# The modulation products of a two-layer diffusion step: thinner beside mLSTM heads 2 to 4, the rest beside the next stage, weights in two tiles of their own

## The chip, the cores and the metric

One core of one Trainium2 chip runs the whole program in one launch. The metric is device time in microseconds, from runs of the same program: the median of three runs before is 1559.02 us (1558.22 to 1560.73). One further execution was taken by the hardware profiler; all views below are of that one.

## The reference

Two layers of a hybrid backbone over 1024 latent tokens and 128 context tokens, model width 1024, all in float32. Layer 0 has four mLSTM heads (two directions, chunks of 128 tokens) and eight grouped-query attention heads from one input projection; layer 1 has 16 heads of 2-D neighbourhood attention. Around each layer stand RMS norms with a shift, a scale and a gate that come from a conditioning vector, one for the latent tokens (`c`) and one for the context (`c_ctx`):

```
m = jnp.dot(jax.nn.silu(cvec), w) + b          # w: (1024, 3072) for each layer
sh, sc, gt = jnp.split(m, 3, axis=-1)
h = rmsnorm(x, g_pre) * (1.0 + sc) + sh
x = x + gt * rmsnorm(y, g_post)
```

Shift and scale of layer 0 are needed before the first projection. The other four vectors (gate of layer 0; shift, scale and gate of layer 1), for both conditioning vectors, are needed only after layer 0's attention. They are what this case is about: 4 x 1024 outputs, each a product of 1024 weights with the vector, twice.

## The kernel before, in words

**Stages.** `run` opens one phase after the other: "front" (norm of the input, first shift and scale, first projections of head 1), "a" (gates of the mLSTM, rest of head 1's projections, first two of head 2), "mlstm" (four heads), "g" (silu gates of the attention heads, keys, values and queries), "gqa" (attention), "out0" (output projection of layer 0, norm into layer 1), "na" (layer 1 and its output). Activations are kept transposed in 9 x 2 tiles as a high and a low part; a projection is 8 blocks of the width times 3 matmuls (high x high, low x high, high x low) into one accumulator bank (`feat_part`, L371 to L373), for one of three chunks of 384 tokens at a time. Two banks (`pj`) take turns, so a projection can start only when the one two before it has been read out.

**The mLSTM phase.** Head by head: `mlstm` runs the recurrence over 8 chunks in both directions (`kw` on POOL in L670, two matmuls in L673, the state's update on VectorE in L680), then three groups of three chunks with the decays (`e`, L653 to L658), the scores and values (L710 to L719), the norm of the result (L725 to L739) and its gating (L750). Between two heads `blocks` projects for the next ones: of head h+1 the values, the output gate and the silu gate, of head h+2 the queries and keys; that is 9 and 6 projections, three to each. The silu gate takes a half-step on ScalarE (L395), one on POOL (L396) and a product on VectorE that reads the bank (L397). The start state of a head is copied in L638 (`mlstm_start`).

**The modulation products.** `mods_rest` is a generator. A step loads 256 rows of the transposed weights (`wm`, 128 x 2 x 512, 512 KB, on SP's queue, L238) and makes four products with sums on VectorE (L252; the sum is read out by a second instruction of the same line), two blocks of rows by two conditioning vectors, which lie broadcast in `cb` (L245). 32 steps cover two halves of the width, 16 each; the load for a step is issued one step ahead. `blocks` asks the generator for a step after every projection, so that the steps come beside heads 2 and 3 and the first of head 4. After the 32nd step the ends follow at once: `mod` sums the halves (L256), `mod_end` adds the bias, applies gains, and for the two gates transposes on PE (L225) and stores rows to DRAM (`ggd`, L228).

**Memory.** Most tiles come from one pool of 35 slots of 4.6 KB per partition (`u`): the 18 activation tiles, queries, keys, values and gates of the heads in work, high and low parts of projection weights, and `wm`. Each phase has a pool of its own (`t`), laid on the memory of the phase before it; a tile there waits only for the tiles that it lies on (`reuse_waits="tile"`). `("e", 3, ...)` and `("nr", 3, ...)` are made first in their phases.

**Order.** The program is written in the order above, and the framework plans the order on each engine and queue from it (`schedule_with_timeline_sim=True`): an instruction can come earlier than its place when its inputs and its tile are ready. Only PE's order in the attention of "gqa" and in the last products of `na_pair` is written out by hand.

**Phase "g".** `zb` projects four blocks of the silu gate, three chunks each, into `gz`, which goes to DRAM; `gqa_kv` projects and normalises keys and values token block by token block (`norm_rope`, tile `nr`, L785 to L791; `key_stack`, L808 to L810), `gqa_q` the queries, twice.

Of the kernel before, what the change touches and what calls it, by code (L numbers as in the profile page):

```python
# [13 lines left out]
ALU = mybir.AluOpType  # L14
# [4 lines left out]
P = 128  # L19
D = 1024  # L20
KB = D // P
T = 1152
NT = 9
NC = 3
CW = 384
# [14 lines left out]
class Kern:  # L40
# [186 lines left out]
            nc.vector.tensor_copy(rows, pt[:16, :P])  # L227
            nc.sync.dma_start(self.ggd[l].rearrange("k r p -> (k r) p"), rows)  # L228

    def mods_rest(self):  # L230

        nc, a = self.nc, self.a
        mp = self.const([P, 2, 4, KB, 2], "mp")
        junk = self.t("mj", 1, [P, 512])

        def load(hf, q):
            w = self.u([P, 2, 512], n="wm")
            nc.sync.dma_start(w.rearrange("p b k -> p (b k)"), a["w_modT"][hf, q])  # L238
            return w

        steps = [(hf, q) for hf in range(2) for q in range(16)]
        nxt = load(0, 0)
        for hf in range(2):
            cb = self.t("cb", 1, [P, 2, 512])
            nc.sync.dma_start(cb.rearrange("p r (k f) -> p r k f", f=P), self.csd.rearrange("(o r k) f -> o r k f", o=1, r=2)[:, :, 4 * hf : 4 * hf + 4, :].to_broadcast([P, 2, 4, P]))  # L245
            for q in range(16):
                w = nxt
                if 16 * hf + q < 31:
                    nxt = load(*steps[16 * hf + q + 1])
                for b in range(2):  # L250
                    for r in range(2):
                        nc.vector.tensor_tensor_reduce(junk, w[:, b, :], cb[:, r, :], 1.0, 0.0, ALU.mult, ALU.add, mp[:, hf, q // 4, 2 * (q % 4) + b, r : r + 1])  # L252
                yield
        for j, (l, kind) in enumerate(((0, 2), (1, 0), (1, 1), (1, 2))):
            m = self.const([P, KB, 2], f"mod{l}{kind}")
            nc.vector.tensor_tensor(m, mp[:, 0, j], mp[:, 1, j], ALU.add)  # L256
            self.mod_end(m, l, kind)
            if kind < 2:
                (self.shift, self.scale)[kind][l] = m
# [623 lines left out]
                nc.vector.tensor_tensor(lo, x, hi.bitcast(F32), ALU.subtract)  # L883
        return Q, ahead

    def zb(self, h):
        nc, a = self.nc, self.a
        for j in range(4):
            gz = self.u([P, T], n="gz")
            w = self.weights(a["w_ab"][20 + j], "lo")  # L890
            if j == 2:
                self.gqa_tables()
            if j == 3:
                ahead = self.gqa_weights(0)
            self.feat(h, w, lambda c, ps: self.silu_gate(gz[:, c * CW : (c + 1) * CW], ps))
            nc.scalar.dma_start(self.gzd[j], gz)
        return ahead

# [391 lines left out]
    def run(self):  # L1290
        nc, a = self.nc, self.a
        x = lambda i: a["x_sample"][i * P : (i + 1) * P, :] if i < 8 else a["x_prompt"]
        rest = iter(())

        def blocks(hd, evs, bs, new=None):
            for b in bs:
                w = self.weights(a["w_ab"][5 * hd + b], new=new)
                for c in range(NC):
                    self.feat(h, w, evs[b], [c])
                    next(rest, None)  # L1300

        with self.phase("front"):
            self.setup()
# [5 lines left out]
            h = [self.chunk("h") for _ in range(NC)]  # L1309
# [80 lines left out]
        with self.phase("mlstm", ("e", 3, [P, 4, CW])):  # L1390
            self.ts = [self.decays_load(0, g) for g in range(NC)]
            start = self.mlstm_start(0)
            rest = self.mods_rest()
            for hd in range(HA):
                self.mlstm(hd, *start, *pr())
                if hd < HA - 1:
# [6 lines left out]
            for _ in rest:  # L1403
                pass
        with self.phase("g", ("nr", 3, [P, 3, 256])):
            w = self.gqa_kv(h, self.zb(h))
            Q, early = [], []
            for g in range(2):
                q, w = self.gqa_q(h, g, w, Q, early)
                Q.append(q)  # L1410
        gz, w = w, []
        with self.phase("gqa"):
            self.pt = self.ring("pt", 14)
# [4 lines left out]
        h = []  # L1418
# [216 lines left out]
```

## Time and profile before

| | us |
|---|---|
| median of three runs (lowest to highest) | 1559.02 (1558.22 to 1560.73) |
| the profiled execution | 1557.34 |
| its span, first to last instruction | 1555.5 |
| PE busy | 1501.9 |
| VectorE (DVE) busy | 852.4 |
| ScalarE (ACT) busy | 653.9 |
| GpSimd (POOL) busy | 605.0 |
| products' first instruction, 128 of them, busy | 110.7 |

The profile gives for each engine how long it was busy, for groups of equal instructions how often they ran and how long one took, and what ended the idle time before them (`<-`, with the engine, tile and line that released it). PEld is the loading of weights into TensorE, which overlaps its matmuls. Stretches are given as start and end in us from the span's start; behind the busy times stand PE's granted clock as a share of full speed, the DMA engines' busy share and GB/s.

### The profile page before, as it was taken

The numbers are of one execution on the slowest core, as the hardware profiler recorded it, in microseconds if no ns is written. First come the engines' busy times: TensorE is split into PE (matmuls) and PEld (weight loads), VectorE is DVE, ScalarE is ACT, GpSimd is POOL, SyncE is SP. The second block draws the span as 40 slices with busy tenths as digits, with TensorE's granted clock in tenths as the row PEclk, the third lists the DMA queues.
The fourth block names the chain that finished last, engine by engine and source line by source line (L and its number), as shares of the span: only waits on it lengthen the run. The fifth ranks groups of instructions, "written<-read, shape, count | busy, mean of one in ns | idle before, by whom it ended". The sixth has DMA issues, their size and how long they took to land.

```text
span 1555.5 us, 27151 instructions
## 1 busy us (share of the span) xinstructions
PE 1501.9 (97%) x10164; PEld 1378.2 (89%) x10164; DVE 852.4 (55%) x2346; ACT 653.9 (42%) x1573; POOL 605.0 (39%) x826
## 2 busy tenths in 40 slices
PE   7899989999999899999999999999999999999998
PEld 5799988999999887777788989999999999989886
DVE  5732897974547946676465452435243434345532
ACT  4622212222235767787344452445243434355411
POOL 3414644644445835675123332333142314243200
PEclk9999999999999999999999999999999999999999
DMA  9112534432221000121334212131213121225342
GB/s 361 74 42 100 218 126 170 163 106 78 99 97 32 16 23 32 37 95 30 102 119 148 89 52 82 39 104 25 92 44 97 31 84 37 88 75 155 123 130 81
DMA packets 75011, 143.80 MB, mean 92 GB/s; under 512 B 15928, under 2 KB 46848, under 8 KB 74880
## 3 DMA queue, kind: packets, MB, share of 16 engines
q1 hardware_dynamic: 70294, 126.91, 24.5%
q10 hardware_dynamic: 4586, 15.16, 2.6%
q8 instruction: 80, 1.31, 0.3%
q14 instruction: 51, 0.42, 0.1%
HBM read 115.47 MB, written 21.86 MB: 88 GB/s over the span
## 4 chain that ended last, share of the span: by engine, by line
PE 83%; DVE 7%; ACT 3%; issue 2%; POOL 2%; DMA 1%; SPq 0%; DVEq 0%; POOLq 0%; ACTq 0%
PE pj L371 12%; PE pj L373 12%; PE pj L372 12%; PE pj L387 7%; PE pj L386 7%; PE pj L388 7%; PE ptr L106 4%; PE o L1285 4%; PE s L1262 3%; PE o L954 3%; PE tr L106 3%; PE s L914 3%; DVE mj L252 2%; PE pj L106 2%; DVE pr L915 1%
## 5 line engine op out<-in xcount | busy, mean ns | idle before, releaser
L371 PE MATMUL pj<-hh,whi 128*128 128x384 f32 x1168 | 399.6, 342 | 4.1 <-DVE z L397 3.8
L373 PE MATMUL pj<-hh,wlo 128*128 128x384 f32 x1168 | 396.4, 340 | 0.0
L372 PE MATMUL pj<-hl,whi 128*128 128x384 f32 x1168 | 395.6, 339 | 0.0
L371 PEld LDWEIGHTS pj<-hh,whi 128*128 128x128 f32 x1168 | 219.5, 188 | 7.3 <-DVE z L397 2.9
L372 PEld LDWEIGHTS pj<-hl,whi 128*128 128x128 f32 x1168 | 219.6, 188 | 1.3
L373 PEld LDWEIGHTS pj<-hh,wlo 128*128 128x128 f32 x1168 | 219.3, 188 | 1.2 <-issue 0.5
L115 POOL TENSOR_TENSOR wlo<-raw,whi 128x1024 fp32r<-128x1024 f32 (+1 forms) x71 | 146.6, 2075 | 155.2 <-ACT whi L114 124.4
L1272 POOL TENSOR_SCALAR sb<-sb,sm 128x512 f32<-128x512 f32 (+1 forms) x128 | 84.8, 668 | 241.2 <-DVE sm L1271 232.7
L924 POOL TENSOR_SCALAR pr<-pr,smg 128x384 f32<-128x384 f32 x192 | 113.8, 611 | 83.2 <-DVE smg L922 57.5
L386 PE MATMUL pj<-whi,hh 128*128 128x256 f32 x432 | 122.4, 284 | 0.3 <-DVE nr L789 0.3
L387 PE MATMUL pj<-wlo,hh 128*128 128x256 f32 x432 | 122.4, 284 | 0.0
L388 PE MATMUL pj<-whi,hl 128*128 128x256 f32 x432 | 122.4, 284 | 0.0
L386 PE MATMUL pj<-whi,yh 128*128 128x512 f32 x288 | 114.2, 397 | 1.5 <-DVE o L1080 1.5
L915 DVE CUSTOM_DVE_ANT_0 pr<-s,zero 128x384 f32<-128x384 f32 x192 | 102.2, 552 | 24.2 <-PE s L914 23.2
L387 PE MATMUL pj<-wlo,yh 128*128 128x512 f32 x288 | 113.8, 395 | 0.0
L388 PE MATMUL pj<-whi,yl 128*128 128x512 f32 x288 | 113.5, 395 | 0.0
L252 DVE CUSTOM_DVE_ANT_0 mj<-wm,cb 128x512 f32<-128x512 f32 x128 | 110.7, 865 | 3.8 <-DMA wm<-in_w_modT_dram 1.8
L1270 ACT ACTIVATE sb<-sb,sm 128x512 f32<-128x512 f32 (+1 forms) x128 | 88.9, 695 | 52.0 <-DVE sm L1268 47.5
L914 PE MATMUL s<-Kst,Q 128*128 128x384 f32 x384 | 105.4, 370 | 4.6 <-DVE smg L915 3.7
L114 ACT CAST whi<-raw 128x1024 fp32r<-128x1024 f32 (+1 forms) x89 | 80.8, 929 | 21.0 <-DMA raw<-in_w_out_dram 6.2
L1268 DVE CUSTOM_DVE_ANT_1 sb<-s,bias 128x512 f32<-128x512 f32 (+1 forms) x112 | 73.0, 664 | 24.3 <-PE ptr L106 11.3
L921 ACT ACTIVATE pr<-pr,smg 128x1152 f32<-128x1152 f32 x64 | 81.0, 1265 | 4.6 <-DVE smg L919 4.1
(351 smaller groups left out, 2961.5 us busy)
## 6 DMA issues: line engine op xcount, KB each, us to landing
wm<-in_w_modT_dram SPq DMA_DIRECT2D x32, 512.0 KB, 5.9
raw<-in_w_c_dram SPq DMA_DIRECT2D x25, 512.0 KB, 3.6
raw<-in_w_ab_dram SPq DMA_DIRECT2D x20, 512.0 KB, 3.5
e<-rbd ACTq DMA_DIRECT2D x12, 768.0 KB, 6.5
bias<-in_na_bias_dram SPq DMA_DIRECT2D x16, 576.0 KB, 5.0
wm<-in_w_mod_dram SPq DMA_DIRECT2D x16, 512.0 KB, 7.1
raw<-in_w_out_dram SPq DMA_DIRECT2D x16, 512.0 KB, 3.6
y<-yd SPq DMA_DIRECT2D x18, 448.0 KB, 3.4
```

Of the source, the lines that this page charges most:

```text
L106: self.nc.tensor.transpose(out, in_, self.ident)
L115: (eng_lo or nc.gpsimd).tensor_tensor(lo, src, hi.bitcast(F32), ALU.subtract)
L252: nc.vector.tensor_tensor_reduce(junk, w[:, b, :], cb[:, r, :], 1.0, 0.0, ALU.mult, ALU.add, mp[:, hf, q // 4, 2 * (q % 4) + b, r : r + 1])
L371: nc.tensor.matmul(ps[:, :CW], a, hh, start=k == 0, stop=False)
L372: nc.tensor.matmul(ps[:, :CW], a, hl, start=False, stop=False)
L373: nc.tensor.matmul(ps[:, :CW], b, hh, start=False, stop=k == KB - 1)
L386: nc.tensor.matmul(ps[:, :width], hh, a, start=k == 0, stop=False)
L387: nc.tensor.matmul(ps[:, :width], hh, b, start=False, stop=False)
L388: nc.tensor.matmul(ps[:, :width], hl, a, start=False, stop=k == KB - 1)
L914: nc.tensor.matmul(s[:, :CW], x, y, start=part == 0, stop=part == 1)
L915: nc.vector.tensor_tensor_reduce(pr[:, c, :], s[:, :CW], zero, -1.0, -NEG, ALU.add, ALU.min, m3[:, c : c + 1])
L924: nc.gpsimd.tensor_scalar(pr[:, c, :], pr[:, c, :], r, 1.0, ALU.mult, ALU.mult)
```

## The change

`blocks` counts its projections in `self.tick` and asks for a step only when the count modulo 8 is under 5. The mLSTM phase gets steps 0 to 23, the phase "g" steps 24 to 31: there `zb` asks for one after the second and third chunk of each of its four blocks. The weights no longer take a slot for each step: two tiles, `wm0` and `wm1`, are made once and take turns, in the mLSTM phase from the slots, in "g" from that phase's own pool, as are `mj` (the products, which nobody reads) and `cb`, which is loaded once more there. The partial sums `mp` are made before the loop. The ends become a function of their own, `mods_end`, which is called after both groups of queries; its body is the old one.

```diff
-    def mods_rest(self):
+    def mods_rest(self, steps, new):
         nc, a = self.nc, self.a
-        mp = self.const([P, 2, 4, KB, 2], "mp")
+        mp = self.mp
         junk = self.t("mj", 1, [P, 512])
-
-        def load(hf, q):
-            w = self.u([P, 2, 512], n="wm")
-            nc.sync.dma_start(w.rearrange("p b k -> p (b k)"), a["w_modT"][hf, q])
+        ring = [new(f"wm{j}") for j in range(2)]
+
+        def load(s):
+            w = ring[s % 2]
+            nc.sync.dma_start(w.rearrange("p b k -> p (b k)"), a["w_modT"][s // 16, s % 16])
             return w
-        steps = [(hf, q) for hf in range(2) for q in range(16)]
-        nxt = load(0, 0)
-        for hf in range(2):
-            cb = self.t("cb", 1, [P, 2, 512])
-            nc.sync.dma_start(cb...)
-            for q in range(16):
-                w = nxt
-                if 16 * hf + q < 31:
-                    nxt = load(*steps[16 * hf + q + 1])
-                for b in range(2):
-                    for r in range(2):
-                        nc.vector.tensor_tensor_reduce(junk, w[:, b, :], cb[:, r, :], ...)
-                yield
+        nxt, old = load(steps[0]), None
+        for s in steps:
+            hf, q = divmod(s, 16)
+            if hf != old:
+                cb, old = self.t("cb", 1, [P, 2, 512]), hf
+                nc.sync.dma_start(cb...)
+            w = nxt
+            if s + 1 in steps:
+                nxt = load(s + 1)
+            for b in range(2):
+                for r in range(2):
+                    nc.vector.tensor_tensor_reduce(junk, w[:, b, :], cb[:, r, :], ...)
+            yield
+
+    def mods_end(self):
+        nc, mp = self.nc, self.mp
         for j, (l, kind) in enumerate(((0, 2), (1, 0), (1, 1), (1, 2))):
...
-    def zb(self, h):
+    def zb(self, h, rest):
...
-            self.feat(h, w, lambda c, ps: self.silu_gate(gz[:, c * CW : (c + 1) * CW], ps))
+            for c in range(NC):
+                self.feat(h, w, lambda c, ps: self.silu_gate(gz[:, c * CW : (c + 1) * CW], ps), [c])
+                if c:
+                    next(rest, None)
...
-        rest = iter(())
+        rest, self.tick = iter(()), 0
...
                     self.feat(h, w, evs[b], [c])
-                    next(rest, None)
+                    self.tick += 1
+                    if self.tick % 8 < 5:
+                        next(rest, None)
...
-            rest = self.mods_rest()
+            self.mp = self.const([P, 2, 4, KB, 2], "mp")
+            rest = self.mods_rest(range(24), lambda n: self.u([P, 2, 512], n=n))
...
         with self.phase("g", ("nr", 3, [P, 3, 256])):
-            w = self.gqa_kv(h, self.zb(h))
+            rest = self.mods_rest(range(24, 32), lambda n: self.t(n, 1, [P, 2, 512]))
+            w = self.gqa_kv(h, self.zb(h, rest))
+            for _ in rest:
+                pass
             Q, early = [], []
             for g in range(2):
                 q, w = self.gqa_q(h, g, w, Q, early)
                 Q.append(q)
+            self.mods_end()
```

More of the change, by code (lines that the diff above doesn't have):

```diff
@@ L228, in mod_end @@
             nc.sync.dma_start(self.ggd[l].rearrange("k r p -> (k r) p"), rows)
-    def mods_rest(self):
+    def mods_rest(self, steps, new):
         nc, a = self.nc, self.a
-        mp = self.const([P, 2, 4, KB, 2], "mp")
+        mp = self.mp
         junk = self.t("mj", 1, [P, 512])
-        def load(hf, q):
-            w = self.u([P, 2, 512], n="wm")
-            nc.sync.dma_start(w.rearrange("p b k -> p (b k)"), a["w_modT"][hf, q])
-            return w
-        steps = [(hf, q) for hf in range(2) for q in range(16)]
-        nxt = load(0, 0)
-        for hf in range(2):
-            cb = self.t("cb", 1, [P, 2, 512])
-            nc.sync.dma_start(cb.rearrange("p r (k f) -> p r k f", f=P), self.csd.rearrange("(o r k) f -> o r k f", o=1, r=2)[:, :, 4 * hf : 4 * hf + 4, :].to_broadcast([P, 2, 4, P]))
-            for q in range(16):
-                w = nxt
-                if 16 * hf + q < 31:
-                    nxt = load(*steps[16 * hf + q + 1])
-                for b in range(2):
-                    for r in range(2):
-                        nc.vector.tensor_tensor_reduce(junk, w[:, b, :], cb[:, r, :], 1.0, 0.0, ALU.mult, ALU.add, mp[:, hf, q // 4, 2 * (q % 4) + b, r : r + 1])
-                yield
+        ring = [new(f"wm{j}") for j in range(2)]
+        def load(s):
+            w = ring[s % 2]
+            nc.sync.dma_start(w.rearrange("p b k -> p (b k)"), a["w_modT"][s // 16, s % 16])
+            return w
+        nxt, old = load(steps[0]), None
[3 more added lines that the diff above has]
+                cb, old = self.t("cb", 1, [P, 2, 512]), hf
+                nc.sync.dma_start(cb.rearrange("p r (k f) -> p r k f", f=P), self.csd.rearrange("(o r k) f -> o r k f", o=1, r=2)[:, :, 4 * hf : 4 * hf + 4, :].to_broadcast([P, 2, 4, P]))
+            w = nxt
[3 more added lines that the diff above has]
+                for r in range(2):
+                    nc.vector.tensor_tensor_reduce(junk, w[:, b, :], cb[:, r, :], 1.0, 0.0, ALU.mult, ALU.add, mp[:, hf, q // 4, 2 * (q % 4) + b, r : r + 1])
+            yield
+    def mods_end(self):
+        nc, mp = self.nc, self.mp
         for j, (l, kind) in enumerate(((0, 2), (1, 0), (1, 1), (1, 2))):
```

## The prediction

> **What bounds the kernel now.** I read the page's totals first, then the busy time of each engine in stretches, cut where the start state of a head is copied (L638), then the products alone in the same stretches, then who waited for whom. The page, totals and the span in 40 slices:
>
> ```profile
> span 1555.5 us, 27151 instructions
> PE 1501.9 (97%) x10164; PEld 1378.2 (89%) x10164; DVE 852.4 (55%) x2346; ACT 653.9 (42%) x1573; POOL 605.0 (39%) x826
> PE   7899989999999899999999999999999999999998
> DVE  5732897974547946676465452435243434345532
> ```
>
> TensorE sets the end: it idles 53.6 us of the whole span (1555.5 - 1501.9), so no change elsewhere can give more. VectorE is at 55% over the span, but its slices 4 to 8 (155 to 350 us) hold 9, 7, 9, 7, 4: that is where the products are. The copies that part the stretches, then busy time in them (PE, PEld, DVE, ACT, POOL, PE's granted clock), and below it the products' first instruction alone:
>
> ```profile
> 148.94 0.49 DVE L638 COPY cs<-ptr 128x128 f32<-128x128 f32 x2 [1.83 <-PE ptr L106]
> ...
> 206.25 0.48 DVE L638 COPY cs<-ptr 128x128 f32<-128x128 f32 x2
> ...
> 294.36 0.48 DVE L638 COPY cs<-ptr 128x128 f32<-128x128 f32 x2
> ...
> 375.55 0.49 DVE L638 COPY cs<-ptr 128x128 f32<-128x128 f32 x2 [2.23 <-PE ptr L106]
> ```
>
> ```profile
> 149.20:206.30 57.10, 52.57 (x332) 50.75 (x333) 47.20 (x115) 12.57 (x39) 36.97 (x44) 0.98 0.46 167
> 206.30:294.40 88.10, 81.63 (x512) 79.81 (x511) 78.12 (x189) 18.34 (x50) 46.85 (x53) 1.00 0.47 169
> 294.40:375.80 81.40, 78.54 (x502) 77.39 (x501) 59.43 (x150) 18.08 (x50) 40.03 (x47) 1.00 0.33 116
> 375.80:447.00 71.20, 71.20 (x462) 71.03 (x461) 31.98 (x67) 15.66 (x49) 27.32 (x47) 1.00 0.27 95
> ```
>
> ```profile
> 149.20:206.30 57.10, 28.81 (x32) 0.98 0.46 167
> 206.30:294.40 88.10, 52.25 (x60) 1.00 0.47 169
> 294.40:375.80 81.40, 29.65 (x38) 1.00 0.33 116
> ```
>
> PE idles 4.53, 6.47, 2.86 and 0.00 us in the four, 13.86 together. A step is four products, so they hold 8, 15, 9.5 and 0 steps: **0.57, 0.43 and 0.30 us of PE idle for each step**. The second and third stretch do the same kind of work (512 and 502 matmuls); the one with 15 steps took 88.10 us, the one with 9.5 took 81.40. And in the third, the part after its last product (the first row has the first and last start) has no idle at all:
>
> ```profile
> L252 DVE CUSTOM_DVE_ANT_0 mj<-wm,cb x128: 673/692/2877, 158.8 to 342.2; 128x512 f32<-128x512 f32 x128
> ...
> 342.90:375.80 32.90, 32.90 (x216) 32.58 (x215) 16.39 (x36) 10.69 (x35) 21.11 (x27) 1.00 0.25 90
> ```
>
> What ended PE's idle time between 110 and 550 us, the longest (total, times, longest):
>
> ```profile
> PE pj L371 <- DVE z L397: 3.8, 3, 1.9
> PE o L673 <- POOL kw L670: 2.4, 2, 1.2
> PE tr L106 <- POOL hs L739: 2.1, 2, 1.3
> ```
>
> A projection waits for its accumulator bank, which the silu gate's product on VectorE empties (L397): that wait belongs to a VectorE that is behind. The two on POOL would stay, except as far as POOL is itself held up (below).
>
> **The change, part by part.** A step's price on VectorE, from the groups between 150 and 350 us (busy, mean ns), two products that follow each other undisturbed, and the weight loads (time from issue to landing):
>
> ```profile
> L252 DVE CUSTOM_DVE_ANT_0 mj<-wm,cb 128x512 f32<-128x512 f32 x128 | 110.7, 865 | 3.8 <-DMA wm<-in_w_modT_dram 1.8
> L252 DVE DVE_READ_ACCUMULATOR2_ANT mp<- 128x1 f32 x128 | 10.1, 79 | 0.0
> ...
> 223.39 0.69 DVE L252 CUSTOM_DVE_ANT_0 mj<-wm,cb 128x512 f32<-128x512 f32 x1
> 224.13 0.69 DVE L252 CUSTOM_DVE_ANT_0 mj<-wm,cb 128x512 f32<-128x512 f32 x1
> ...
> DMA to landing us min/median/max: 4.2/5.9/8.8
> ```
>
> Undisturbed, one product follows another after 0.74 us, so a step is 4 x 0.74 = 2.96; by the means it is 4 x (0.865 + 0.079) = 3.78.
>
> *Thinner steps beside heads 2 to 4.* The counter starts at 9 when the stage begins (3 + 6 projections in the stage before it), and a remainder under 5 of 8 lets a step pass. So the three stretches get 6, 9 and 9 steps in place of 8, 15 and 9.5 (by program place 9, 15 and 8). At the third stretch's price, 24 x 0.30 = 7.2 us of idle remain of 13.86: **-6.7**. I take that price because all three new densities (6 in 57, 9 in 82, 9 in 81 us) are nearest to that stretch's. The bounds: no idle at all, as after 342.9, gives -13.9; the first stretch's price gives 24 x 0.57 = 13.7, so -0.2.
>
> *Eight steps beside the next stage's gate projections* (two of three chunks of four blocks). In 375.8 to 447 VectorE is busy 31.98 of 71.20 us and PE never idles; eight steps are 8 x 2.96 = 23.7 and fit into the 39.2 that are free. Nothing can be gained where PE is never idle, so the lower bound is 0; the upper is worked out under the second rival (9.7). I take the price of the third stretch again, 8 x 0.30 = **+2.4**.
>
> [...] The row first: a product at 241.06 met POOL's low-half subtraction and took 2.88 us, and POOL's half-step of the silu gate (L396) is longer beside the products (149 to 294 us) than without them (376 to 447):
>
> ```profile
> 240.97 2.42 POOL L115 TENSOR_TENSOR wlo<-raw,whi 128x1024 fp32r<-128x1024 f32 x1 [0.24 <-ACT whi L114]
> 241.06 2.88 DVE L252 CUSTOM_DVE_ANT_0 mj<-wm,cb 128x512 f32<-128x512 f32 x1
> ...
> L396 POOL TENSOR_SCALAR th<-th 128x384 f32<-128x384 f32 x5 | 4.1, 821 | 5.7 <-ACT th L395 5.7
> L396 POOL TENSOR_SCALAR th<-th 128x384 f32<-128x384 f32 x14 | 7.9, 565 | 30.4 <-ACT th L395 29.0 <-issue 1.3
> ```
>
> [...]
>
> *Two tiles of their own.* The weights leave the 35 shared slots. Two waits for a slot by projection weights go, both off PE (who waited, for whom; total, times, longest):
>
> ```profile
> POOL wlo L115 <- DVE mp L252: 5.1, 1, 5.1
> ACT whi L114 <- DVE mp L252: 4.2, 2, 3.2
> ```
>
> In return two slots are held through the stage, which the old order held only when a load was near, and load s+1 may now start only when step s-1 is done: two steps in 5.9 + 2.96 us, 4.4 us each. That is under the time from one projection to the next, as the counts of L371, eight to a projection, give it: 57.10 us for 8.5 in the first stretch (6.7 each), 71.20 for 13 in the last (5.5 each):
>
> ```profile
> 149.20:206.30 57.10, 23.32 (x68) 12.82 (x69) 0.98 0.46 167
> 375.80:447.00 71.20, 35.25 (x104) 19.36 (x103) 1.00 0.27 95
> ```
>
> I cost it at nothing, hidden by that spacing; if the spacing is gone VectorE waits up to 1.8 us at a time, as it did once above, with the gates behind it. The loads stay on SP's queue. Eight of them, and a third load of the broadcast vector, now come between the loads of the gate and key weights, where the DMA engines are 27% busy (the last stretch above) against 33 to 47% where they were: nothing, unless one waits there for its tile with weights behind it, which is the first rival.
>
> *The ends (`mods_end`) move behind the queries.* All issued there before too: four sums, four bias sums, two gains and one scale on VectorE, two transposes on PE, two row copies and two stores on SP. The groups (min/median/max ns, first to last start) and the stretch where they now come:
>
> ```profile
> L256 DVE TENSOR_TENSOR mod<-mp x4: 163/396/1454, 284.4 to 345.5; 128x16 f32<-128x16 f32 x4
> L225 PE MATMUL ptr<-cc,mod x2: 270/270/270, 367.9 to 371.7; 128*16 128x128 f32 x2
> ...
> 530.00:550.00 20.00, 15.99 (x101) 13.92 (x102) 12.68 (x47) 14.20 (x39) 12.43 (x22) 0.83 0.01 2
> ```
>
> PE idles 4.0 us there anyway and VectorE 7.3. I take 0, between 0 and 1.5 (two chains of three instructions of 0.16 us and a transpose of 0.27, all waited for). What reads them comes a whole stage later.
>
> **Sum:** -6.7 + 2.4 = -4.3 us. The profiled execution took 1557.34 us (its span is 1.84 less) and the three runs' median is 1559.02: 1553.0 and **1554.7**.
>
> **The rivals.** *Late steps (slower).* The next stage's product, weight and vector tiles are new tiles of that stage, made after its three `nr` (3 x 3 KB). If its memory begins where the mLSTM stage's did, they lie on the second and third `e` (three of 6 KB) and on `kw`, `cf`, `ct`, `hs` behind them. The last reads of those in the fourth head, and the first use of `nr`:
>
> ```profile
> L717 PE MATMUL s<-v,e x144: 271/275/422, 143.5 to 423.7; 128*128 128x129 f32 x144
> L106 PE MATMUL tr<-cc,hs x9: 271/272/275, 420.9 to 434.2; 128*128 128x128 f32 x9
> 447.10 0.29 DVE L785 TENSOR_TENSOR nr<-pj,rope 128x128 f32<-128x128 f32 x1 [1.65 <-ACT nr L782]
> 447.00:475.00 28.00, 28.00 (x238) 27.87 (x238) 18.82 (x74) 13.95 (x69) 12.78 (x29) 1.00 0.16 55
> ```
>
> Then the loads start at 424 to 434, land 5.9 later, and eight steps of 4.4 us run from about 440 to 475: 6.4 steps, 18.9 us, beside keys and values that already take 18.82 of VectorE's 28. That is 9.7 too much, in front of PE: -6.7 + 9.7 = +3.0, 1562.0. It decides from 5.4 steps after 447 (9.2 us free are 3.1 steps, 6.7 us saved are 2.3 more). For it: those rows. Against: where the memory lies isn't in the trace.
>
> *The steps run ahead.* The first sum of L256 ran at 284.4, when 12 steps that precede it in the program were still to come (the last product is at 342.2): the planner runs early what is ready. Without slots to wait for, 24 steps could run at 4.4 us each and be done by 265, as dense as before: 24 x 0.5 (between 0.43 and 0.57) = 12.0, so -1.9 + 2.4 = +0.5, 1559.5. Against: so far the steps kept to the projections (8 steps to 8.5).
>
> *All idle goes*, because undisturbed steps fill only gaps: -13.9, 1545.1. For it: no idle in 342.9 to 447. Against: the waits for POOL above aren't the products' alone.
>
> **How the numbers follow.** Forecast 0.45, late steps 0.22, run ahead 0.20, all idle gone 0.10; 0.03 for an order that the planner makes worse elsewhere. 0.2% is 3.1 us, about what can be told from no change here. The forecast's own range, 1551.5 to 1557.5, gives 0.36 faster and 0.09 same; late steps 0.12 slower and 0.10 same; run ahead 0.04 faster, 0.11 same, 0.05 slower. Faster 0.50, same 0.30, slower 0.20. The range 1546.5 to 1562.5 leaves out half of the last rival and the upper part of the first.
>
> **What would show it.** Right: PE idle under 8 us from 149 to 376, no VectorE slice of 9 there, no wait of L371 for L397 over 1 us. The first rival: products of the next stage after 447, and PE idle between 447 and 475, where now there is none. The second: the 24th step before 280 us and VectorE at 9 until then. I am wrong altogether if PE idle from 149 to 376 stays at 13 us while steps are evenly spread: then they weren't its cause.

## The result, and the profile after

The changed kernel takes **1569.58 us** (median of 5 runs, 1565.99 to 1572.64) against 1559.02 for the kernel before (5 runs beside it, 1556.66 to 1560.73): a ratio of **1.0063, 95% interval 1.0045 to 1.0080**. It is slower, by 10 us where 4 us less were forecast. The page of the changed kernel, totals and the slices that answer to those shown of before:

```profile
span 1567.8 us, 27127 instructions
PE 1505.9 (96%) x10164; PEld 1380.2 (88%) x10164; DVE 849.0 (54%) x2346; ACT 652.4 (42%) x1573; POOL 607.4 (39%) x826
PE   7899888999999999999999999999999999999998
DVE  5732898725478856677365442435243534345632
```

VectorE does no more than before (849.0 and 852.4 us), PE 4.0 us more with the same 10164 matmuls, and 61.9 us of PE's span are idle in place of 53.6. The dense slices of VectorE are still there (157 to 313 us: 8, 9, 8, 7), and behind them one that is nearly bare (2). (Line numbers are each kernel's own.) The busy times of the changed kernel in the stretches between the copies of the start states (first three rows), to the first normalised key (fourth), to the first output of the attention (fifth) and to the end; behind the times of PE, PEld, DVE, ACT and POOL stand PE's granted clock, the DMA share and GB/s. Below it the same for the kernel before, the first three stretches in one row, the later two as they are:

```profile
149.31:209.19 59.88, 51.98 (x326) 50.37 (x327) 48.73 (x117) 12.69 (x40) 39.20 (x46) 0.97 0.45 154
209.19:301.11 91.92, 81.91 (x500) 79.86 (x500) 79.33 (x198) 17.94 (x50) 44.32 (x48) 0.96 0.47 153
301.11:380.94 79.83, 79.29 (x507) 78.59 (x506) 30.98 (x63) 17.29 (x50) 35.42 (x47) 1.00 0.24 80
380.94:452.80 71.86, 71.86 (x468) 71.73 (x467) 39.55 (x88) 16.70 (x46) 28.59 (x48) 1.00 0.37 127
452.80:574.00 121.20, 113.56 (x890) 105.52 (x889) 97.14 (x340) 68.52 (x289) 70.38 (x117) 0.97 0.15 47
574.00:1567.80 993.80, 975.07 (x6642) 877.27 (x6642) 479.60 (x1346) 461.96 (x983) 339.86 (x451) 1.00 0.25 79
```

```profile
149.20:375.80 226.60, 212.74 (x1342) 207.95 (x1343) 184.75 (x448) 48.99 (x139) 123.84 (x142) 0.99 0.42 150
446.60:562.90 116.30, 111.66 (x887) 106.04 (x886) 82.12 (x288) 70.10 (x289) 65.65 (x117) 0.97 0.09 30
562.90:1555.50 992.60, 974.41 (x6642) 876.30 (x6642) 479.54 (x1346) 461.97 (x983) 338.58 (x451) 1.00 0.25 79
```

The spans differ by 12.3 us, and these rows hold all of it but 1.2 in front of or between them. Beside heads 2 to 4 the three stretches now take 231.63 us (59.88 + 91.92 + 79.83) for 226.60: **+5.0**. PE idles 7.90 + 10.01 + 0.54 = 18.45 us there, before 13.86. Keys, values and queries take 121.20 for 116.30: **+4.9**. From the attention on it is **+1.2**. Where the products went, in nearly the same cuts:

```profile
149.31:209.19 59.88, 29.99 (x33) 0.97 0.45 154
209.19:301.11 91.92, 54.93 (x63) 0.96 0.47 153
301.11:380.94 79.83, 0.00 (x0) 1.00 0.24 80
380.94:453.00 72.06, 7.74 (x11) 1.00 0.37 128
453.00:500.00 47.00, 14.71 (x22) 1.00 0.25 81
```

The 24 steps that the program spreads over three stretches all ran in the first two (8.25 and 15.75 steps, as dense as before), none in the third. Of the eight late steps 2.75 ran beside the gates and 5.25 behind them, beside keys and values (one product lies on the cut and counts in both of the last two rows). What ended PE's idle time from 149 to 292 us in the changed kernel (total, times, longest), VectorE around its longest wait, and PE's first matmul behind that wait:

```profile
PE s L721 <- DVE e L715: 4.4, 1, 4.4
PE tr L106 <- POOL hs L743: 3.2, 3, 1.3
PE o L677 <- DVE cs L684: 2.6, 2, 2.2
```

```profile
240.76 0.69 DVE L253 CUSTOM_DVE_ANT_0 mj<-wm,cb 128x512 f32<-128x512 f32 x1 [0.69 <-DMA wm<-in_w_modT_dram]
...
247.88 0.89 DVE L253 CUSTOM_DVE_ANT_0 mj<-wm,cb 128x512 f32<-128x512 f32 x1 [3.62 <-DMA cb<-csd]
...
248.70 0.94 DVE L715 TENSOR_TENSOR e<-e,s 128x768 f32<-128x768 f32 x1
```

```profile
249.70 0.80 PE L721 MATMUL s<-v,e 128*128 128x129 f32 x2 [4.35 <-DVE e L715]
```

Before, the longest wait there was 1.9 us. Here VectorE runs product after product ahead of the projections, catches up with the loads (0.69 us behind `wm` at 240.76), reaches the second half's first step at 244.26 (247.88 - 3.62) and stands 3.62 us behind the load of the broadcast vector `cb`. The score product `e` (L715), which PE needs, stands behind it in VectorE's order. PE's wait also costs afterwards. The same kernel in stretches of 4 us:

```profile
244.00:248.00 4.00, 1.21 (x9) 0.80 (x7) 0.38 (x2) 1.42 (x2) 2.83 (x3) 0.90 0.65 245
248.00:252.00 4.00, 2.30 (x9) 2.30 (x10) 3.96 (x11) 0.00 (x0) 0.22 (x1) 0.50 0.40 151
252.00:256.00 4.00, 4.00 (x24) 4.00 (x22) 2.24 (x7) 1.36 (x2) 0.76 (x2) 0.74 0.46 131
```

Behind the 4.35 us the granted clock is 0.50 and then 0.74, so by an estimate from these rows some 2 us more are lost while PE counts as busy (1.15 of 2.30, and 1.04 of 4.00).

### The profile page after: what moved, and what is told of

It reads as the page before. It is cut to its first block, busy times and chain, and to the rows that moved or that the text cites. A ratio compares the mean times of both kernels' runs of the same rounds, so it can differ in the third digit from the quotient of the medians.

```text
span 1567.8 us, 27127 instructions
## 1 busy us (share of the span) xinstructions
PE 1505.9 (96%) x10164; PEld 1380.2 (88%) x10164; DVE 849.0 (54%) x2346; ACT 652.4 (42%) x1573; POOL 607.4 (39%) x826
## 4 chain that ended last, share of the span: by engine, by line
PE 76%; DVE 9%; issue 4%; DMA 4%; POOL 4%; ACT 3%; SPq 0%; POOLq 0%; DVEq 0%; ACTq 0%
PE pj L375 10%; PE pj L377 10%; PE pj L376 10%; PE pj L390 7%; PE pj L391 7%; PE pj L392 7%; PE ptr L106 4%; PE o L1292 4%; PE s L1269 3%; PE o L961 3%; PE tr L106 3%; PE s L921 3%; DVE mj L253 2%; PE pj L106 2%; DMA wm<-in_w_mod_dram 1%
## 5 line engine op out<-in xcount | busy, mean ns | idle before, releaser
L253 DVE CUSTOM_DVE_ANT_0 mj<-wm,cb 128x512 f32<-128x512 f32 x128 | 107.4, 839 | 12.6 <-DMA cb<-csd 7.0
L390 PEld LDWEIGHTS pj<-whi,hh 128*128 128x128 f32 x432 | 81.2, 188 | 6.4 <-ACT V L852 3.4
```

The source lines that it names most:

```text
L390: nc.tensor.matmul(ps[:, :width], hh, a, start=k == 0, stop=False)
```

## The experiments

Each was timed in five rounds against the kernel before; a ratio stands with its 95% interval. "Stretches" are those between the four copies of start states, 226.60 us before with 13.86 us of PE idle (14.12 when they are cut exactly at the copies' starts, as in the runs below). Each edit was planned anew by the framework, so the order of other instructions can differ too; no run takes the products out of an order that stays as it was.

### The parts of the change

**The thinning alone** (`slots_24`): the changed kernel with a slot for each step and without the late ones.

```diff
-        ring = [new(f"wm{j}") for j in range(2)]
+        ring = [new(f"wm{j}") for j in range(2)] if steps[0] else []
-            w = ring[s % 2]
+            w = new("wm") if s < 24 else ring[s % 2]
...
-            rest = self.mods_rest(range(24, 32), lambda n: self.t(n, 1, [P, 2, 512]))
+            rest = iter(())
```

> The forecast's first term alone: 24 steps beside heads 2 to 4, paced 7, 9, 8 by a slot each, the last eight steps left out (their sums count as zero). The forecast had 7.2 us of idle there, 6.7 less than before: 1552 to 1554. By the runs since (24 such steps left 13.5 to 15.7 us idle, with the late steps or the gate steps beside them) thinning wins nothing: 1558.5 to 1562.

1558.99 us (before 1558.58), ratio 0.9994 (0.9980 to 1.0009). With slots the steps do keep to the projections: 28, 36 and 32 products in the three stretches. The stretches in one row, and what PE waited for most in them:

```profile
150.72:376.58 225.86, 212.97 (x1330) 208.17 (x1331) 166.44 (x380) 47.91 (x139) 122.23 (x140) 0.98 0.37 131
```

```profile
PE tr L106 <- POOL hs L743: 7.9, 5, 2.7
```

Fewer and evenly spread steps leave 12.89 us of PE idle for 13.86, not 7.2. The waits of projections for VectorE's silu product (3.8 us before) are gone, but waits for the norm `hs` on POOL have grown from 2.1 to 7.9 us. **Thinning by itself wins nothing.**

**With the late steps** (`slots_thin`): the same, but the eight late steps run as in the changed kernel, so of the diff above only the first two edits.

```diff
+        ring = [new(f"wm{j}") for j in range(2)] if steps[0] else []
+            w = new("wm") if s < 24 else ring[s % 2]
```

> The changed kernel with one edit: the 24 steps beside the heads take a slot each, as before; thinning, the eight steps of the next stage and the late ends stay. Theory one: the steps keep to the projections (7, 9 and 8 beside the three stretches), the fourth head's start state comes 6 to 10 us earlier than in the changed kernel (371 to 375), and the time is 1560 to 1564. Theory two: no difference to the changed kernel, 1569. The first sum of the prediction (the thinner steps alone save 6.7) would give 1557 to 1559 with the late steps kept.

1566.28 us, ratio 1.0041 (1.0028 to 1.0053). The 24 steps lie as in `slots_24` (28, 36 and 32 products), and PE idles 15.70 us there (228.79 - 213.09), so the 12.89 above is no gain that can be told from 13.86. The last stage's row answers to 121.20 of the changed kernel and 116.30 before:

```profile
449.80:571.20 121.40, 113.89 (x890) 105.90 (x889) 97.06 (x340) 68.65 (x289) 70.35 (x117) 0.97 0.15 47
```

**Without the late steps, tiles kept** (`g_out`):

```diff
-            rest = self.mods_rest(range(24, 32), lambda n: self.t(n, 1, [P, 2, 512]))
+            rest = iter(())
```

> The changed kernel with the eight steps of the next stage left out: a quarter of the modulation sums is not computed (they count as zero), so its time stands for the changed kernel without those steps. If the late steps beside keys and values cost what the stages' starts say (4.8 us from the first key to the attention): 1564 to 1565. If they cost nothing: 1569. If they are the whole loss: 1559.

1566.59 us, ratio 1.0048 (1.0031 to 1.0066). Keys to queries take 116.80 us again:

```profile
454.90:571.70 116.80, 112.18 (x890) 106.30 (x889) 82.70 (x291) 70.25 (x289) 65.82 (x117) 0.97 0.10 30
```

So the late steps cost 4.4 us in that stage, and the moved ends, which are still behind the queries here, at most the 0.5 to 116.30.

**The two tiles alone** (`ring_only`), in the kernel before:

```diff
+        ring = [self.u([P, 2, 512], n=f"wm{j}") for j in range(2)]
-            w = self.u([P, 2, 512], n="wm")
+            w = ring[q % 2]
```

> The kernel before with one edit: the weights of the products in two tiles that take turns, made once, in place of one slot for each step; 32 steps at every projection, ends where they were. Theory one (the two tiles free the products from the wait for slots, so that VectorE runs them earlier, in front of loads that have not landed, and the heads wait behind them): slower than before by 3 to 7 us, 1562 to 1566, more products before the third head's start state than the 92 of before, and waits of VectorE for weight loads of some us in all. Theory two (the tiles are harmless, the loss comes from the steps that moved to the next stage): 1559, as before.

1573.47 us, ratio 1.0086 (1.0073 to 1.0098): dearer than the whole change. First and second stretch, before 57.10 and 88.10 us at a clock of 0.98 and 1.00:

```profile
148.53:208.71 60.18, 53.32 (x325) 51.98 (x326) 48.65 (x116) 12.83 (x40) 39.26 (x46) 0.94 0.44 152
208.71:308.97 100.26, 90.28 (x530) 88.07 (x528) 87.77 (x215) 18.16 (x50) 49.68 (x51) 0.93 0.49 162
```

This edit alone lets the products run ahead: 33, 72 and 23 of them in the three stretches, for 32, 60 and 38 before (by the prediction's rows, which count a product on a cut twice). So the slot for each step had been a brake, and tiles that take turns take it off. How a slot brakes isn't shown; the loads wait longer on SP's queue for earlier products with two tiles (78.9 us from 149 to 376 in the changed kernel) than with slots (26.7 in the kernel before), so it isn't simply that wait.

**Three tiles** (`ring3`):

```diff
-        ring = [new(f"wm{j}") for j in range(2)]
+        ring = [new(f"wm{j}") for j in range(3)]
-            w = ring[s % 2]
+            w = ring[s % 3]
```

> The changed kernel with three weight tiles taking turns in place of two, still loaded one step ahead; the order of the products on VectorE is nearly that of the changed kernel (32 and 96 products ahead of the second and third head's state copies). If VectorE standing in its order behind a load of a tile just emptied is what cost time in the first two stretches, the wait of VectorE for weights goes there, PE idles about 5 and 6.5 us there in place of 7.9 and 10.0, and the run takes 1563 to 1566. If the density of steps that run ahead is enough by itself, idle stays at 7 to 8 and 9 to 11 and the run takes 1568 to 1571.

1569.77 us, ratio 1.0066 (1.0050 to 1.0081), no change. VectorE no longer waits for `wm` in its longest waits (for `cb` 2.6 us); PE still idles 5.54 and 12.13 us in the first two stretches. That the ring was too short isn't the cause, and the third slot that is held costs nothing that can be told.

**Both broadcast vectors at the start** (`cb_two`), so that the 3.62 us wait has nothing to wait for:

```diff
+        for hf in sorted({s // 16 for s in steps}):
+            cb = cbs[hf] = self.t("cb", 1, [P, 2, 512]) if not cbs else self.u([P, 2, 512], n="cb")
+            nc.sync.dma_start(cb...)
-            if hf != old:
-                cb, old = self.t("cb", 1, [P, 2, 512]), hf
-                nc.sync.dma_start(cb...)
+            w, cb = nxt, cbs[hf]
```

> The changed kernel with the broadcast vectors of both halves loaded at the stage's start, the second in a slot of the common pool, so that no product has to wait for the second half's load; the products' order is nearly the same (31 and 96 ahead of the second and third state copies, for 33 and 96). If VectorE's 3.6 us behind that load cost what PE's trace shows right behind it (4.35 us idle, and a clock of 0.50 and 0.74 in the 8 us after), the second stretch is 4 to 6 us shorter and the run takes 1563.5 to 1566. If running ahead costs by itself, VectorE is late elsewhere instead: 1567.5 to 1571.

1567.77 us, ratio 1.0052 (1.0035 to 1.0070), not to be told from the change itself. That wait is gone, and others have taken its place: the second stretch takes 83.34 us for 91.92, the third 86.68 for 79.83, all three 231.70 for 231.63. PE's longest from 149 to 310 us:

```profile
PE tr L106 <- POOL hs L744: 6.5, 4, 3.6
```

So taking this wait away wins nothing: by these runs it was one form of a VectorE that is late, not the cost itself.

**The late steps moved in front of the stage's end** (`zb_inside`): the gate blocks come inside the mLSTM stage and all 32 steps, thinned, take slots.

```diff
-            w = ring[s % 2]
+            w = self.u([P, 2, 512], n="wm")
-            rest = self.mods_rest(range(24), ...)
+            rest = self.mods_rest(range(32), None)
...
+            wg = self.zb(h, rest)
             for _ in rest:
                 pass
         with self.phase("g", ...):
-            w = self.gqa_kv(h, self.zb(h, rest))
+            w = self.gqa_kv(h, wg)
```

> The changed kernel with the gate projections moved into the mLSTM phase and a slot for each step, so that no tile of the next stage has to wait for memory and the products keep to the projections; thinning, 24 + 8 steps and late ends stay. Theory one with late steps as the second cause: both losses go and the thinning is worth what the prediction said, 1550 to 1556. If the thinning itself is worth nothing: 1558 to 1560. If the late ends cost most: 1565 or more.

1563.42 us, ratio 1.0024 (1.0011 to 1.0038). Keys to queries are back at 116.3 us, but the gates took 74.37 us with 2.06 us of idle, where PE had had none:

```profile
380.23:454.60 74.37, 72.31 (x468) 71.64 (x467) 53.01 (x129) 16.18 (x47) 31.80 (x48) 1.00 0.41 140
```

**The ends back in front** (`zb_inside_ends`): the run before with `self.mods_end()` behind the last step.

```diff
+            self.mods_end()
         with self.phase("g", ...):
...
-            self.mods_end()
```

> The run with the gate blocks inside the mLSTM phase (1563.4), with one difference: the ends (sums, biases, the two transposes of gates) come right behind the last step, before keys and values, in place of behind the queries. If the moved ends cost nothing, as predicted (0 to 1.5 us), the time stays at 1562 to 1564.5. If their place behind the queries holds PE up where the attention begins, it falls to 1559 to 1561.5, and the stretch from the first y on is 2 us shorter.

1565.25 us, ratio 1.0037 (1.0020 to 1.0055): nothing won. The place of the ends doesn't matter within what can be told.

### What the products cost at all

**None** (`no_products`) and **half** (`half`), in the kernel before:

```diff
-                for b in range(2):
-                    for r in range(2):
-                        nc.vector.tensor_tensor_reduce(junk, w[:, b, :], cb[:, r, :], ...)
```

```diff
-                    for r in range(2):
+                    for r in range(1):
```

> The kernel before with all 128 modulation products left out (their sums count as zero; the loads of weights and of the broadcast vector stay), so that VectorE has 121 us less to do from 149 to 342 us. If the products cause PE's idle time beside heads 2 to 4 (the forecast's premise), the 13.9 to 14.1 us of idle from 149 to 376 fall to under 4 and the run takes 1546 to 1550. If they aren't its cause (the other reading of the runs so far, where 24 evenly spread steps left 13.5 to 15.7 us idle), 10 us or more stay and the run takes 1555 to 1559. In between, their share is what is missing: 1 us less of time for 1 us less of idle.

> The kernel before with only the latent conditioning vector's products (64 of 128; the context's sums count as zero), all weight loads kept. All products left out brought 14.1 us (1559.0 to 1544.95). If the cost is VectorE's time in front of other work, in proportion, half of it goes and the run takes 1551 to 1553.5. If VectorE had slack and only the crowded places cost, three quarters go: 1547 to 1550. If the weight loads and their slots cost most, it is over 1555, but the run without products, which kept the loads, speaks against it.

Without products 1544.95 us, ratio 0.9906 (0.9891 to 0.9921): **14.1 us** (12.3 to 17.0 by the interval; the two profiled executions differ by 11.5), about the most that any placing can win. With half of them 1557.91 us beside 1560.35, ratio 0.9991 (0.9975 to 1.0006): nothing. The stretches in one row, of the run without products first, then of that with half:

```profile
150.74:362.14 211.40, 209.27 (x1332) 207.37 (x1333) 80.00 (x179) 48.71 (x139) 103.00 (x140) 0.99 0.44 158
```

```profile
153.37:379.80 226.43, 212.62 (x1332) 208.64 (x1333) 142.03 (x318) 48.86 (x139) 113.50 (x140) 0.98 0.42 150
```

PE idles 2.13 us without products and 13.81 with 64 of them, as with 128 (13.86). (The profiled execution of `half` took 1563.59 us, 5.7 above the median of its runs; 4.4 us of it came in front of the stretches, whose first copy is at 153.37 for 148.94.) POOL, which has the same work in all three (140 to 142 instructions), is busy 103.00, 113.50 and 123.84 us: the products make its instructions longer. The same group of POOL without products and with all of them (the state's keys `kw`, 46 instructions each, busy and mean ns):

```profile
L668 POOL TENSOR_TENSOR kw<-k,nat 128x128 f32<-128x128 f32 x46 | 17.3, 399 | 64.7 <-PE o L671 64.7
```

```profile
L670 POOL TENSOR_TENSOR kw<-k,nat 128x128 f32<-128x128 f32 x46 | 24.2, 546 | 62.4 <-PE o L673 62.4
```

**Short products** (`short`), 64 columns of 512:

```diff
-    nc.vector.tensor_tensor_reduce(junk, w[:, b, :], cb[:, r, :], ...)
+    nc.vector.tensor_tensor_reduce(junk[:, :64], w[:, b, :64], cb[:, r, :64], ...)
```

> The kernel before with products over 64 of the 512 columns (7/8 of every sum left out); the loads, the tiles, the number of products and their places stay (40, 100 and 128 products ahead of the second, third and fourth state copies; before 32, 91, 128). Half the products cost as much as all (226.4 and 226.6 us for the three stretches; 211.4 without any). If the length of a product (0.69 us alone, up to 2.9 beside POOL) is what puts VectorE's other work late, the short ones cost little: the stretches take 213 to 217 us, PE idles 3 to 6 us there and the run takes 1546 to 1550. If it is their mere presence (tiles held until they are read, VectorE's order, a wait for a load at its head), the stretches stay at 224 us or more and the run at 1556 or more.

1551.67 us, ratio 0.9951 (0.9932 to 0.9970): 7.6 of the 14.1 us go, which is between the two expectations.

```profile
149.59:368.51 218.92, 210.79 (x1332) 206.94 (x1333) 130.04 (x447) 48.46 (x139) 102.13 (x140) 0.99 0.42 155
```

POOL is back at 102.13 us, as without products, and still PE idles 8.13 us. So about half of the cost goes with the products' length, lengthened POOL work included; the other half comes with 128 products in VectorE's order that are short (0.41 us in the mean, 0.23 in the median), and with their loads.

**Products without loads** (`no_loads`): one weight tile for all steps.

```diff
-                if 16 * hf + q < 31:
-                    nxt = load(*steps[16 * hf + q + 1])
```

> The kernel before with one weight tile, loaded once, that all 32 steps read (so the sums are those of the first step's weights): 31 loads of 512 KB left out, all 128 products at nearly the same places (34, 105, 128 ahead of the second, third, fourth state copies). If the loads are what costs (they take the DMA engines from the decay load of 768 KB, at whose head VectorE, GpSimd and ScalarE wait), the three stretches shrink from 226.6 to 216 us or less and the run takes 1546 to 1551. If VectorE's time for the products is what costs, the stretches stay at 222 to 228 us and the run takes 1555 to 1560.

1560.25 us, ratio 1.0009 (0.9999 to 1.0020). The DMA engines are half as busy (0.23 for 0.42) and nothing is won:

```profile
149.51:378.10 228.59, 214.78 (x1334) 209.80 (x1335) 183.04 (x446) 47.71 (x139) 121.59 (x140) 0.98 0.23 77
```

**In the kernel before the cost is the products on VectorE, not their loads.**

### Steps elsewhere

**One stage earlier** (`early_a`): the generator starts with stage "a", whose projections ask for steps too; its tiles take slots.

```diff
         with self.phase("a"):
+            rest = self.mods_rest()
...
                     later(c, (b,))
+                    next(rest, None)
```

> The kernel before with the generator started one stage earlier, where between 78 and 149 us PE is at 9.8 of 10 and VectorE at 3.3 of 10: 13 steps now come there, 5 in the first stretch, 14 in the second, none in the third (counted from VectorE's order: 52, 73 and 128 products ahead of the second, third... state copies). The ends stay behind the last step; a product, vector and weight tile each take a slot of the common pool. If a step costs by the work that it lies beside (nothing beside plain projections, 0.43 to 0.57 us of PE idle beside a head's recurrence and norms), the idle of the three stretches falls from 14.1 to about 9 (5 x 0.57 + 14 x 0.43 = 8.9), and the run takes 1553 to 1555.5. If a step costs 14.1/32 = 0.44 us wherever it lies, the time stays at 1558 to 1560. If the stage before can't take them (slots or loads late in front of the first head), that stage gets 3 us longer or more and the run takes 1561 or more.

1562.20 us beside 1560.35, ratio 1.0006 (0.9991 to 1.0020). The idle of the three stretches fell to 10.6 us (9 expected), and the time did not: 1.8 us of idle came in the stage before, and the clock in the first stretch fell to 0.88. The first two stretches:

```profile
150.64:205.74 55.10, 50.90 (x304) 48.77 (x305) 42.19 (x90) 12.54 (x38) 37.41 (x46) 0.88 0.50 173
205.74:299.34 93.60, 87.36 (x535) 85.30 (x534) 76.68 (x195) 19.84 (x55) 46.62 (x56) 0.98 0.34 120
```

**Earlier and later** (`early_late`): stage "a", the blocks of head 4, and the gates inside the mLSTM stage.

```diff
+                    if give:
                         next(rest, None)
...
-                    blocks(hd + 1, evs, (2, 3, 4))
+                    blocks(hd + 1, evs, (2, 3, 4), give=hd == 2)
-                        blocks(hd + 2, evs, (0, 1))
+                        blocks(hd + 2, evs, (0, 1), give=False)
```

> All 32 steps in slots, but none beside head 2 and the recurrences of heads 1 and 2 as far as the program asks: 13 in the stage before (52 products ahead of the first state copy), 7 to 10 beside the blocks of head 4, the rest spread over the twelve gate chunks, which come inside the mLSTM stage (92 products ahead of the first gate, 128 behind the last). If a step costs nothing beside plain projections and where it lies beside recurrence and norms sets the price, idle is near 0.5 and 1.6 us in the first two stretches as without products, 2 to 3 in the third, 2 to 4 beside the gates and 2 more in the stage before: 5 to 6 us less than before, 1552.5 to 1555.5. If steps cost alike everywhere, or the slower clock behind PE's gaps takes it back as it did with the generator one stage earlier (1562.2 against 1560.4), it is 1558 to 1562.

1561.41 us, ratio 1.0013 (1.0001 to 1.0025). The second stretch, free of products, takes 79.09 us for 88.11 and idles 0.12; the third, with 6.5 steps, pays it back:

```profile
205.18:284.27 79.09, 78.97 (x505) 78.28 (x504) 29.09 (x63) 18.13 (x50) 35.43 (x48) 1.00 0.23 82
284.27:375.54 91.27, 85.27 (x532) 84.31 (x531) 53.76 (x118) 19.61 (x52) 44.63 (x50) 0.96 0.34 121
```

One wait makes most of it. VectorE and ScalarE there:

```profile
353.75 0.96 DVE L706 TENSOR_TENSOR e<-e,qT 128x768 f32<-128x768 f32 x1 [5.44 <-DMA e<-rbd]
354.63 1.83 DVE L733 TENSOR_TENSOR hs<-hs,hb 128x384 f32<-128x384 f32 x1
```

```profile
356.56 0.31 ACT L736 ACTIVATE hb<-hs 128x128 f32<-128x128 f32 x1 [9.13 <-DVE hs L733]
...
357.45 0.46 ACT L101 COPY v<-ptr 128x384 f32<-128x384 f32 x1
```

A decay load (issued at 345.27, landed 8.5 us later, for 4.9 in the median in the kernel before, from 149 to 376) holds the head of VectorE; behind it waits the norm `hs`, behind that ScalarE's `hb`, and behind that the copy `v` that empties PE's transposition bank: PE stands 5.69 us. Five loads of 512 KB were issued just ahead of it, from 342.41 to 344.68, three of them weights of steps and one `cb`, and the DMA engines were 0.92 busy until it landed. So here, other than in `no_loads`, the steps' loads may have their part in the wait; that wasn't tested.

**Beside layer 1** (`na8`): 12 steps in stage "a", 2 behind the first state copy, 10 beside the gates, and the eight of layer 1's gate, in `mods_rest(range(12, 16))`, beside the neighbourhood attention of layer 1.

```diff
+                if p == 0:
+                    rest = self.mods_rest(range(12, 16))
                 if p < 7:
                     for j, _ in enumerate(unit):
...
+                        if j in (2, 6):
+                            next(rest, None)
```

> All 32 steps, but next to none beside heads 2 to 4: 12 in the stage before the heads, 2 behind the first state copy, 10 beside the gate chunks (inside the mLSTM stage), and the 8 of layer 1's gate beside the neighbourhood attention of layer 1, with the last ends there. If the place beside recurrence and norms sets the price, the three stretches take 211 to 215 us as without products (before 226.6); the stage before costs 1.5 to 2 more, the gates 2 to 3, the attention of layer 1 0 to 3: 1549 to 1554, faster than both kernels. If steps cost alike wherever they lie, 0.44 us each, it takes 1557 to 1561.

1567.67 us, ratio 1.0061 (1.0042 to 1.0081), as slow as the change. Heads 2 to 4 (first row) are 10.7 us shorter, near what they take without products. The gates (second, before 71.05) and the attention of layer 1 (third, 675.00 us before, as the row below it shows) take it back with 6.9 and 11.8 us:

```profile
149.89:365.83 215.94, 212.99 (x1344) 210.27 (x1345) 92.56 (x198) 51.02 (x142) 111.46 (x150) 0.98 0.22 77
365.83:443.80 77.97, 74.55 (x468) 73.13 (x467) 61.40 (x156) 16.27 (x47) 33.76 (x48) 0.98 0.45 152
758.00:1444.80 686.80, 675.40 (x4623) 631.25 (x4622) 332.92 (x834) 291.24 (x661) 219.40 (x246) 1.00 0.28 86
```

```profile
760.30:1435.30 675.00, 670.42 (x4621) 630.35 (x4620) 302.98 (x766) 291.39 (x661) 215.00 (x245) 1.00 0.25 80
```

Eight steps with the last ends, 30 us of VectorE's work (332.92 - 302.98) put into 675 us in which it was 45% busy, go with 11.8 us more in this one execution, 6.8 of them idle time of PE (11.40 for 4.58). That is 1.5 us for each step, by its row the dearest place of all. No version that computes everything beats the kernel before.

## Why the prediction was wrong

**What held.** PE sets the end, and the products are what makes it wait: without them its idle beside heads 2 to 4 goes from 13.86 to 2.13 us. The bound "no idle at all, -13.9" was about right (-14.1 by the medians), though for some part by luck: 2.13 us of idle stay, and the profiled executions differ by 11.5 us. The sentence at the prediction's end, that idle staying at 13 us with evenly spread steps would mean they weren't its cause, came half true: with 24 even steps 12.89 us stayed, and yet they were the cause.

**The step that failed: a price for each step.** Term 1 divided a stretch's idle by its steps (0.57, 0.43, 0.30) and multiplied by the new count. That reads a proportion into three rows which the runs don't have. 128 products, 96 even ones and 64 leave 13.86, 12.89 (in another execution 15.70) and 13.81 us of idle; none leaves 2.13. Fewer still, though in other places: 76 in `early_a` leave 10.56, 30 in `early_late` 7.97, 8 in `na8` 2.95. The cost comes with the first steps and hardly grows with the last ones. So 0.30 was no price of a thin step. The third stretch had no idle behind its last product at 342, a part that a mean over the stretch hides; why its products cost less than those of the first two isn't shown. Thinning alone measured 0.9994 (0.9980 to 1.0009), which is -0.9 us (-3.1 to +1.4), where -6.7 stood; the nearest bound, -0.2, was the better value.

**"Two tiles of their own: nothing."** The text asked whether the loads could keep up with the projections, and priced only the case that they couldn't (1.8 us at a time). It missed that the slots were also a brake: with a slot for each step the 24 steps keep to the projections (28, 36 and 32 products in the three stretches), with two tiles the planner's order puts them first (33, 63 and 0). Alone, in the kernel before, the tiles cost 1.0086, 13.4 us. Within the change they cost 3.4 us if the late steps are there (1.0063 - 1.0041) and 8.4 if not (1.0048 - 0.9994); each such difference is uncertain by 3 to 4 us, from the two intervals. Taken one after the other, the steps from the kernel before to the change are -0.9 us for the thinning (`slots_24`), +8.4 for the tiles (`g_out`) and +2.3 for the late steps, +9.8 together, where the sum had -6.7, 0 and +2.4.

**"Eight steps beside the gates: +2.4."** They cost 2.3 us (1.0063 - 1.0048, which alone can't be told from nothing) to 7.3 us (1.0041 - 0.9994) by the times and 4.4 by the stage's own rows (121.20 against 116.80). This is the mechanism of the rival of late steps: the first product ran at 442.25 (forecast "about 440"), the last at 484.1 (475), 5.25 steps beside keys and values (6.4). The size was half of its 9.7, which priced the steps as if VectorE's whole excess stood in front of PE. Steps that did lie beside the gates weren't free either: beside 7 of them PE idled 2.06 us in `zb_inside`, in two waits for the norm `hs`, where it had no idle before. "PE never idles there" was read as room for more; it described the place while VectorE had no products there.

**The rivals.** Running ahead came true as well (the 24th step at 291.2 us, with VectorE's slices at 8 to 9), and it brought more idle, not the 12.0 us forecast for it: 18.45. The prediction gave the two mechanisms 0.20 and 0.22 as if one excluded the other. They came together, and neither alone explains the time; that is also why the range ended at 1562.5.

**The ends**, costed at 0 to 1.5: 0.5 us at most by the stage's row, and nothing that two timed kernels could tell apart. A smaller slip: VectorE's slices from 155 to 350 us hold 8, 9, 7, 9, 7, one place off what the text read, and its waits for a slot are three (1 and 2 in the rows), not two; nothing hung on either.

**POOL beside the products.** The prediction showed a product that took 2.88 us beside a subtraction on POOL, for 0.69 us undisturbed, and half-steps on POOL that took 821 ns beside products and 565 ns without them; its sum has no term for either. The runs show it on a larger scale: POOL's same work takes 20.8 us longer with the products than without (123.84 against 103.00). It should have been weighed for all 32 steps. How the products make these instructions longer isn't shown. How much of PE's idle comes by this way and how much by VectorE's order alone isn't separated either: with short products POOL's loss is gone (102.13 us) and half the cost stays, but these also leave VectorE 54.7 us less to do (184.75 against 130.04).

## What to carry to other kernels

Don't price filler work by idle time per unit, or by the filled engine's free share: ask instead what short chain through that engine the bound engine waits on, since here half of the filler instructions cost as much as all of them. The cheap test is to take the filler out altogether, and then half of it: the first gives the most that any placing can win, the second tells whether thinning can win anything. And before a tile gets buffers of its own, ask what the shared buffers were holding back.

## What the runs showed of the hardware

PE's granted clock was below full behind most of its longer waits, and behind some shorter ones. In all seventeen traces, between 150 us and the fourth state copy, 16 of 17 waits of PE of 2.69 us or longer were followed by 4 us at a mean of 0.50 to 0.67 of full clock (the one of 3.15 us in `slots_thin` by 1.00), and 8 of 21 waits of 1.8 to 2.5 us by 0.57 to 0.66; the other thirteen show 1.00. The shortest of the sixteen, one of the eight and the exception, from `slots_24`, the change and `slots_thin`:

```profile
286.06 0.55 PE L106 MATMUL tr<-cc,hs 128*128 128x128 f32 x3 [2.69 <-POOL hs L743]
```

```profile
171.09 0.68 PE L677 MATMUL o<-v,kw 128*128 128x129 f32 x4 [2.17 <-DVE cs L684]
```

```profile
352.26 0.49 PE L721 MATMUL s<-v,e 128*128 128x129 f32 x2 [3.15 <-DVE e L715]
```

The length of a wait alone doesn't part the two (0.63 behind 1.82 us in `early_a`, 1.00 behind 3.15 us in `slots_thin`), and what does isn't shown. So idle time alone does not rank these kernels: `early_a` idles less than the kernel before from the first state copy to the first key (10.6 us against 14.1) and takes 2.5 us longer there (300.16 against 297.66); the mean clock of its three stretches is 0.96, for 0.99 before. The clock also scatters nearly equal work: up to the gates `g_out` has the change's program but for one `memset` on GpSimd, and their three stretches took 234.70 and 231.63 us, the first two at clocks of 0.93 to 0.94 and of 0.96 to 0.97.
